# Two zero products of 256 columns ahead of the first and the second product of every chunk of a delta-rule recurrence

## Chip, cores, metric

One NeuronCore of a Trainium2 chip runs the whole program, in one launch. The metric is the device time of one execution in microseconds, the median of several; below it is the time of the slowest (here the only) core.

## What is computed

One inference step of a two-layer decoder, for a prompt of 1024 tokens and 8 sample rows. Layer 0 (a convolution branch and a sparse attention branch) is not touched by the change. Layer 1 is RWKV-7 time mixing: per head a 64x64 matrix state S is carried over the tokens.

```python
def rwkv_mixer(x, shift_prev, S0, mu, w_rkvz, w0, w1, w2, a0, a1, a2, k_k, k_a, r_k, gn_g, gn_b, w_out):
    ...
    r, k, v, z = jnp.einsum('nbtd,nde->nbte', xsh[:4], w_rkvz)
    ...
    def step(S, inp):
        r_t, w_t, k_t, v_t, kk_t, a_t = inp
        sa = jnp.einsum('bhvk,bhk->bhv', S, kk_t)
        S = S * w_t[:, :, None, :] - sa[..., None] * (kk_t * a_t)[:, :, None, :] + v_t[..., None] * k_t[:, :, None, :]
        return S, jnp.einsum('bhvk,bhk->bhv', S, r_t)
    S_fin, y = lax.scan(step, S0.astype(f32), (tm(r), tm(decay), tm(k), tm(v), tm(kk), tm(a)))
    ...
    out = (y.reshape(B, T, D_C).astype(x.dtype) * jax.nn.silu(z)) @ w_out
    return out, S_fin, x[:, -1]
```

The layer's output goes through a residual and a layer norm. 16 heads of 64, 1024 tokens.

## The kernel before

Phases A to C (layer 0) fill the first half of the time; phase D (`phase_d`, L1110 to L1883) is layer 1. The kernel is written as one long program in Python; a scheduler then orders the instructions of each engine by when it takes their inputs to be ready, and by their place in the program. TensorE (PE) runs its queue in that order.

Phase D has two kinds of work.

**The recurrence**, in 16 units: `units` is token group g (8 groups of 128 tokens) times half d (the heads in two halves of 8). A unit has two chunks (c = 0, 1) of 64 tokens. `s1` and `s2` prepare a unit's matrices and the pieces of an inverse, `joinUT` puts the inverse `UT` together with small products, and `s3` (L1533) is the serial chain. Per chunk, with the state and values in `SV`:

- L1547, the state products: 8 products `pA<-SV,AM` into the first half of the PSUM tile `pA`; L1549, a copy on VectorE (DVE) takes it out as `E`.
- L1552 and L1554: 8 products `pB<-AM,SV` and 2 products `pB<-SV,ident` start `pB`.
- L1559, the products with the inverse: 8 products `pA<-E,UT` into the second half of `pA`, on top of what is there; L1560 (ScalarE, ACT) and L1561 (DVE) copy the sum into `SV`.
- L1566 and L1568: 8 products `pB<-SV,BK` and 8 products `pB<-MRB,SV`; L1571 (DVE) makes the new state, L1572 (ACT) the output `Y`.

The trace shows all of these with the line of the helper `mm`, L1541, and twice as many records as products. After two chunks a norm follows (`yc` L1577, `sq` L1580, `var` L1585, logarithm and exponential L1586 and L1587, L1588 and L1589), and its result `sq` goes to memory; the last unit's stays on chip as `G.Y`. `pA` and `pB` have one buffer each, in a pool that the norm's `yc` and `var` use too.

**The filler**, generators in the list `F1`: projections `t_proj` (L1195 to L1197), and output projections `t_out` (L1807 to L1809) with the layer norm `ln_out`. `t_last` is the last output projection, for 256 tokens, with products at L1736 to L1738. It splits the weights into a high and a low part (L113 on ACT, L121 on GpSimd (POOL) or DVE), multiplies tile 0 (128 tokens) while the last unit runs, joins it with the residual (L1743) and norms it, waits for `G.Y`, prepares the last rows (`prep`, L1709), and multiplies tile 1 with weights that it kept on chip in the buffers `AM`, `SV`, `BK`, `MRB` of earlier units.

The loop at L1858 advances `s3` by one step, then the other generators, then the filler by `RATE` steps:

```python
            main = s3(g, d, JJ[u])
            for k in range(8):
                step(main)
                ...
                over = run(F1, RATE[u >= 6] - over)
```

So in the text of the program, filler products stand between any two steps of `s3`. A plain product has no tie to them, and the scheduler may issue it ahead of filler that was written before it. `tc.keep_in_program_order(...)` ties an instruction behind the last one of its engine that was written before it, as an order of issue and without a wait. `warm` (L1528) uses it in the last unit alone: after each of the three steps of a chunk, four zero products of 256 columns into a PSUM tile `pg` of their own, which nothing of the chain reads.

## Time and profile before

| | us |
|---|---|
| median of 3 runs | 2153.94 |
| lowest and highest | 2147.12, 2162.48 |
| the profiled execution | 2146.61 |
| its span, first to last instruction | 2144.6 |
| mean granted TensorE clock over the span | 0.889 |

The profile is of one execution. Starts are counted from the first instruction. The engines are PE (products), PEld (its weight loads), DVE, ACT, POOL, and SP, which issues most DMAs. A granted clock of 1.00 is 2.4 GHz and 0.50 is 1.2 GHz. The recurrence begins at about 1256 us; the last unit's first state products stand at 2087.48 us.

### The profile page before, as it was taken

How to read it: one execution, taken by the hardware profiler on the slowest of the kernel's cores; microseconds unless marked ns; L12 is line 12 of the kernel's file. 1: busy time of each engine (PE TensorE's matmuls, PEld its weight loads, DVE VectorE, ACT ScalarE, POOL GpSimd, SP SyncE). 2: the span in 40 equal slices, each digit the busy share in tenths (PEclk: the TensorE clock that was granted, in tenths of full speed). 3: DMA queues.
4: the chain of work that ended last, by engine and by line, in shares of the span. 5: the costliest groups of instructions: out<-in, count | busy, mean ns of one | idle time of the engine just before them, and what ended most of it. 6: DMA issues, size and time to landing. Idle time of an engine off the chain costs nothing. (4 is left out here: it accounts for less than half of the span.)

```text
span 2144.6 us, 41476 instructions
## 1 busy us (share of the span) xinstructions
PE 1826.6 (85%) x16106; PEld 1528.2 (71%) x16106; DVE 1474.2 (69%) x2550; ACT 1144.5 (53%) x2353; POOL 934.3 (44%) x765
## 2 busy tenths in 40 slices
PE   5997997848998998798878899899999886999875
PEld 5896886836776786575767898678688754976654
DVE  5998995467887788425645347873855899466864
ACT  3233224555665556356746555865874467455544
POOL 4667676564655455354534421242344435212211
PEclk9898998958998887798889899979789997999778
DMA  6424334440221112545656534443443445443443
GB/s 241 140 71 148 119 121 172 170 146 19 68 63 49 53 54 65 165 129 156 184 190 197 173 117 106 130 133 115 126 146 126 146 144 166 131 112 103 152 148 101
DMA packets 231519, 273.18 MB, mean 127 GB/s; under 512 B 71481, under 2 KB 171505, under 8 KB 227162
## 3 DMA queue, kind: packets, MB, share of 16 engines
q1 hardware_dynamic: 210136, 213.11, 32.5%
q0 software_dynamic: 7616, 41.52, 5.8%
q10 hardware_dynamic: 13570, 15.90, 2.1%
q8 instruction: 127, 2.08, 0.4%
q14 instruction: 70, 0.57, 0.1%
HBM read 210.37 MB, written 64.27 MB: 128 GB/s over the span
## 5 line engine op out<-in xcount | busy, mean ns | idle before, releaser
L121 POOL TENSOR_TENSOR wl<-w,wh 128x1024 fp32r<-128x1024 f32 x76 | 195.5, 2573 | 341.6 <-ACT wh L113 330.3
L1195 PE MATMUL mm<-xh,wh 128*128 128x256 f32 (+1 forms) x1024 | 308.2, 303 | 20.9 <-ACT og L1330 10.9
L1197 PE MATMUL mm<-xh,wl 128*128 128x256 f32 (+1 forms) x1024 | 300.5, 295 | 4.4 <-POOL wl L121 4.4
L1196 PE MATMUL mm<-xl,wh 128*128 128x256 f32 (+1 forms) x1024 | 302.8, 296 | 1.6 <-POOL xk L1215 0.8
L1195 PEld LDWEIGHTS mm<-xh,wh 128*128 128x128 f32 x1024 | 202.6, 199 | 33.4 <-ACT og L1330 13.7
L113 ACT ACTIVATE wh<-w 128x1024 fp32r<-128x1024 f32 (+1 forms) x122 | 126.0, 1034 | 165.5 <-DMA w<-in_w_fm 60.7
L1197 PEld LDWEIGHTS mm<-xh,wl 128*128 128x128 f32 x1024 | 202.9, 199 | 9.5 <-POOL wl L121 5.6
L1196 PEld LDWEIGHTS mm<-xl,wh 128*128 128x128 f32 x1024 | 204.3, 200 | 5.1 <-issue 2.1
L268 DVE SCALAR_TENSOR_TENSOR c<-U,cw,c 128x1024 f32<-128x1024 f32 x120 | 198.0, 1674 | 0.9
L604 POOL TENSOR_TENSOR Pl<-PT,Ph 128x512 fp32r<-128x512 f32 (+1 forms) x102 | 132.1, 1299 | 145.9 <-DVE Ph L603 114.9
L252 POOL TENSOR_TENSOR cbuf<-cbuf 128x256 f32<-128x256 f32 (+2 forms) x72 | 131.1, 1827 | 85.8 <-ACT cbuf L250 82.9
L217 PE MATMUL S<-xh,wh 128*128 128x344 f32 (+1 forms) x432 | 147.1, 341 | 23.3 <-ACT wh L113 19.3
L219 PE MATMUL S<-xh,wl 128*128 128x344 f32 (+1 forms) x432 | 145.6, 337 | 14.6 <-POOL wl L121 11.2
L218 PE MATMUL S<-xl,wh 128*128 128x344 f32 (+1 forms) x432 | 146.7, 340 | 3.8 <-POOL xl L121 3.7
L1223 POOL TENSOR_TENSOR xl<-xs,xh 128x520 fp32r<-128x520 f32 (+1 forms) x76 | 106.5, 1404 | 82.5 <-ACT xh L1222 80.7
L250 ACT ACTIVATE cbuf<-cbuf,wrow 128x256 f32<-128x256 f32 x192 | 79.3, 495 | 113.3 <-DMA cbuf<-in_ccmp,cix 72.1
L1219 DVE SCALAR_TENSOR_TENSOR xs<-xk,mu,xs 128x512 f32<-128x512 f32 x96 | 94.4, 989 | 55.2 <-ACT xs L1218 54.3
L217 PEld LDWEIGHTS S<-xh,wh 128*128 128x128 f32 (+1 forms) x432 | 85.4, 198 | 25.6 <-ACT wh L113 24.1
L562 DVE TENSOR_REDUCE nm<-S 128x1 f32<-128x640 f32 (+7 forms) x128 | 88.2, 698 | 19.8 <-PE S L558 19.0
L219 PEld LDWEIGHTS S<-xh,wl 128*128 128x128 f32 (+1 forms) x432 | 84.9, 197 | 19.7 <-POOL wl L121 13.4
L602 ACT ACTIVATE PT<-mm 128x512 f32<-128x512 f32 (+1 forms) x102 | 59.4, 586 | 57.9 <-PE mm L590 46.8
L218 PEld LDWEIGHTS S<-xl,wh 128*128 128x128 f32 (+1 forms) x432 | 84.9, 196 | 7.0 <-POOL xl L121 4.5
(666 smaller groups left out, 5305.1 us busy)
## 6 DMA issues: line engine op xcount, KB each, us to landing
w<-in_w_rkvz SPq DMA_DIRECT2D x64, 512.0 KB
w<-in_w_out SPq DMA_DIRECT2D x32, 512.0 KB
w<-in_w_fm SPq DMA_DIRECT2D x25, 512.0 KB
xk<-x1T SPq DMA_DIRECT2D x48, 260.0 KB
xk<-x1T SPq DMA_DIRECT2D x48, 256.0 KB
w<-in_w_out SPq DMA_DIRECT2D x16, 256.0 KB
x<-in_xp SPq DMA_DIRECT2D x8, 512.0 KB
x<-x ACTq DMA_DIRECT2D x8, 512.0 KB
```

Source lines behind the costliest of these rows:

```text
L113: nc.scalar.activation(hi, src, AF.Copy, **({} if scale is None else {"scale": scale}))
L121: e_lo.tensor_tensor(lo, src, hi, op=SUB)
L217: nc.tensor.matmul(dst, lhsT=wh[:, k, 0:n], rhs=xh[:, k, sl], start=k == 0, stop=False)
L218: nc.tensor.matmul(dst, lhsT=wh[:, k, 0:n], rhs=xl[:, k, sl], start=False, stop=False)
L219: nc.tensor.matmul(dst, lhsT=wl[:, k, 0:n], rhs=xh[:, k, sl], start=False, stop=k == 7)
L252: nc.gpsimd.tensor_tensor(bv[:, 0:n], bv[:, 0:n], bv[:, n:2 * n], op=ADD)
L268: e.scalar_tensor_tensor(c[:, i, 0:T], u[:, k:k + T], cwh[:, i, k:k + 1], c[:, i, 0:T], op0=MUL, op1=ADD)
L604: lambda: nc.gpsimd.tensor_tensor(Pl[:, 0:w], PT[:, 0:w], Ph[:, 0:w], op=SUB)]
L1195: nc.tensor.matmul(dst, lhsT=wh[:, k], rhs=xh[k][:, lo:hi], start=k == 0, stop=False)
L1196: nc.tensor.matmul(dst, lhsT=wh[:, k], rhs=xl[k][:, lo:hi], start=False, stop=False)
L1197: nc.tensor.matmul(dst, lhsT=wl[:, k], rhs=xh[k][:, lo:hi], start=False, stop=k == 7)
L1223: (nc.vector if early[0] and k % LD == 0 else nc.gpsimd).tensor_tensor(lo[k][:, 0:n], t[:, 0:n], hi[k][:, 0:n], op=SUB)
```

## The change

A helper `fillw` issues n zero products: `wz` (zeros, bf16, 128 columns of it as weights, 256 columns moved) into the tile that it is given, with `start=True`, each tied behind what was written before it. It is called with n = 2 in each of the 32 chunks at two places: on the first half of `pA` before the state products, and on the second half of `pA` before the products with the inverse. Both sets of products write to the same places after it, so each stands behind its pair. That is 64 pairs, 128 zero products. `wz` is made before `joinUT` now, with 256 columns for 512.

```diff
+        wz = late.tile([128, 256], BF, name="wz")
+        nc.gpsimd.memset(wz, 0.0)
+
+        def fillw(z, n):
+            for _ in range(n):
+                tc.keep_in_program_order(nc.tensor.matmul(z, lhsT=wz[:, 0:128], rhs=wz, start=True, stop=True,
+                                                          skip_group_check=True))
+
         def joinUT(J):
...
-        wz = late.tile([128, 512], BF, name="wz")
-        nc.gpsimd.memset(wz, 0.0)
-
         def warm(n):
...
             for c in range(2):
                 pA = py_.tile([128, 2, 4, 64], F32, name="pA")
                 pB = py_.tile([128, 2, 4, 64], F32, name="pB")
+                fillw(pA[:, 0].rearrange("p m t -> p (m t)"), 2)
                 for m, h, i in MH:
                     mm(pA[h, 0, m], AM[:, m, i, c], SV[:, m, i, c], m == 0)
...
                 if wn:
                     warm(wn)
                 yield
+                fillw(pA[:, 1].rearrange("p m t -> p (m t)"), 2)
                 for m, h, i in MH:
                     mm(pA[h, 1, m], UT[h, 2 * m + c], E[h, m], False)
```

Lines of the changed kernel: `fillw` is L1482, the helper `mm` L1546, `E` L1555, the copies into `SV` L1567 and L1568, the new state L1578, `yc` and `var` L1584 and L1592, `t_last`'s products L1743 to L1745 (so L1743 is a product there and the join of the kernel before; the join is now L1750).

The order of PE changes from the first unit to the end; the first unit's first state products stand in row 5658 before and in row 5876 now, of some 9000. Three places.

PE, second chunk of the second unit, the kernel before (waits in brackets name the engine waited for; `pg` belongs to `joinUT`):

```order
L1541 MATMUL pB<-SV,ident 64x256 x2
L1511 MATMUL pg<-U,AB 32x32 [waits DVE_49,PE_49,Activation_49]
L1511 MATMUL pg<-U,AB 32x32 x14
L1541 MATMUL pA<-E,UT 64x64 [waits DVE_49]
L1541 MATMUL pA<-E,UT 64x64 x7
```

The same kind of place in the changed kernel, with the filler products that stand ahead of it:

```order
L1195 MATMUL mm<-xh,wh 128x264
L1196 MATMUL mm<-xl,wh 128x264
L1482 LDWEIGHTS wz
L1482 MATMUL pA<-wz 128x256 [waits DVE_49]
L1482 LDWEIGHTS wz
L1482 MATMUL pA<-wz 128x256
L1546 MATMUL pA<-E,UT 64x64 x8
```

The wait for the copy `E` has moved from the first product with the inverse to the first zero product. It is so in 27 of the 32 pairs at this place; of the 32 pairs ahead of the state products 9 wait for ACT, 10 for PE itself, and the others for nothing.

PE, the last unit (g = 7, d = 1), the kernel before, from its first state products; `t_last`'s products into `mm` from `MRB` stand behind all that is shown, and behind the unit's norm (`yc` and `var`):

```order
L1585 MATMUL pB<-sq,cc 128x512
L1541 MATMUL pA<-SV,AM 64x64 x8
L1541 MATMUL pB<-AM,SV 64x64 x8
L1541 MATMUL pB<-SV,ident 64x256 x2
...
L1531 MATMUL pg<-wz 128x256
L1541 MATMUL pA<-E,UT 64x64 x8
...
L1541 MATMUL pB<-SV,BK 64x64 x8
L1541 MATMUL pB<-MRB,SV 64x64 x8
```

The changed kernel, the same unit's first products with the inverse:

```order
L1743 MATMUL mm<-MRB,xh 128x512
L1744 MATMUL mm<-MRB,xh 128x512
L1745 MATMUL mm<-MRB,xl 128x512
L1482 LDWEIGHTS wz
L1482 MATMUL pA<-wz 128x256
L1482 LDWEIGHTS wz
L1482 MATMUL pA<-wz 128x256
L1546 MATMUL pA<-E,UT 64x64 x8
```

All 48 products of `t_last`'s tile 0, up to the last pair of weights (in `MRB`), and the 24 of tile 1 that are written with them, now stand ahead of the last unit's first products with the inverse; the unit has its second chunk and the norm still to come. The other 24 products of tile 1 come last in both kernels.

DVE in the changed kernel, the same place, from the split of the last weights on (`big` is the residual, `st` the norm's sums, L1750 the join of tile 0; L1568 and L1578 are the chain's):

```order
L121 TENSOR_TENSOR MRB<-w,MRB 128x1024
L1750 SCALAR_TENSOR_TENSOR big,st<-big,mm 128x512 x2
L1685 TENSOR_SCALAR st<-st 128x1
L1568 COPY SV<-pA 64x4x64
L1690 TENSOR_SCALAR st<-st 128x1
L1698 SCALAR_TENSOR_TENSOR big<-big,st,w 128x1024
L1699 TENSOR_TENSOR st<-st 128x1
L1578 TENSOR_TENSOR SV<-pB,PC 64x4x64 x2
```

The join and a part of the layer norm of tile 0 now stand in the middle of the chain of the last unit; in the kernel before, the join of tile 0 stands behind that chain.

## Rows read from the trace of the kernel before

**Rows 1.** The page's first part: busy time, share, instructions.
```profile
PE 1826.6 (85%) x16106; PEld 1528.2 (71%) x16106; DVE 1474.2 (69%) x2550; ACT 1144.5 (53%) x2353; POOL 934.3 (44%) x765
```

**Rows 2.** Stretches: length, busy of PE, PEld, DVE, ACT, POOL; clock, DMA, GB/s.
```profile
1256.00:1586.00 330.00, 301.83 (x3882) 250.08 (x3879) 240.47 (x471) 229.12 (x496) 99.64 (x114) 0.89 0.43 125
1586.00:1750.00 164.00, 147.98 (x1780) 128.48 (x1779) 112.54 (x199) 85.86 (x178) 67.87 (x53) 0.97 0.47 144
1750.00:2090.00 340.00, 290.44 (x3658) 219.55 (x3658) 241.03 (x497) 198.24 (x400) 84.01 (x71) 0.86 0.43 134
2090.00:2125.00 35.00, 29.05 (x231) 20.01 (x229) 13.27 (x29) 15.19 (x27) 9.46 (x4) 1.00 0.35 113
```

**Rows 3.** Zero products of the last unit: their line, then PE in time.
```profile
L1531 PE MATMUL pg<-wz x24: 272/273/283, 2089.8 to 2106.5; 128*128 128x256 bf16 x24
...
2089.78 0.61 PE L1531 MATMUL pg<-wz 128*128 128x256 bf16 x4
2090.32 0.68 PE L1541 MATMUL pA<-E,UT 64*64 64x64 f32 x16
```

**Rows 4.** The chain's line L1541: records, then idle of PE before it.
```profile
L1541 PE MATMUL pA<-SV,AM x512: 222/222/369, 1270.4 to 2094.9; 128*64 128x64 f32 x171
...
L1541 PE MATMUL pA<-E,UT x512: 216/218/366, 1318.6 to 2101.9; 64*64 64x64 f32 x171
...
  DVE SV L1571: 11.5, 12
  DVE E L1549: 9.8, 7
```

**Rows 5.** PE in time, last unit and tile 0 of the last projection.
```profile
2094.01 1.14 PE L1541 MATMUL pA<-SV,AM 128*64 128x64 f32 x16
...
2096.13 0.61 PE L1531 MATMUL pg<-wz 128*128 128x256 bf16 x4
...
2108.88 1.02 PE L1577 MATMUL pA<-Y,cc 128*128 128x512 f32 x2
...
2122.54 0.39 PE L1736 MATMUL mm<-MRB,xh 128*128 128x512 f32 x1
...
2124.63 0.39 PE L1738 MATMUL mm<-MRB,xl 128*128 128x512 f32 x1
...
2129.39 0.40 PE L1738 MATMUL pa<-MRB,xl 128*128 128x512 f32 x1
```

**Rows 6.** The last weights of tile 0: SP, POOL and ACT in time.
```profile
2108.12 8.26 SPq L1186 DMA_DIRECT2D w<-in_w_out  x3
...
2120.90 1.04 ACT L113 ACTIVATE MRB<-w 128x1024 fp32r<-128x1024 f32 x1
...
2116.61 2.38 POOL L121 TENSOR_TENSOR BK<-w,BK 128x1024 fp32r<-128x1024 f32 x1 [0.58 <-ACT BK L113]
```

**Rows 7.** DVE and ACT in time, from the last unit's result to the end.
```profile
2120.30 0.61 DVE L1709 SCALAR_TENSOR_TENSOR xs<-sq,vec,xs 128x128 f32<-128x128 f32 x2
...
2131.52 0.68 DVE L1743 SCALAR_TENSOR_TENSOR big<-big,sm 128x512 f32<-128x512 f32 x1
...
2133.32 0.68 DVE L1743 SCALAR_TENSOR_TENSOR big<-big,pa 128x512 f32<-128x512 f32 x1
...
2139.29 1.28 DVE L1696 SCALAR_TENSOR_TENSOR big<-big,st,w 128x1024 f32<-128x1024 f32 x1
...
2126.04 1.15 ACT L1680 ACTIVATE og<-big,st 128x1024 bf16<-128x1024 f32 x1 [1.81 <-DVE st L1678]
...
2127.89 1.28 ACT L1685 ACT_TABLE_LOAD   x1
```

**Rows 8.** Stretches at the lower clock and one ahead of them, columns as above.
```profile
1420.00:1437.10 17.10, 16.09 (x128) 11.88 (x126) 14.49 (x28) 13.67 (x32) 6.70 (x8) 0.50 0.29 74
1498.50:1501.90 3.40, 2.04 (x43) 1.71 (x41) 0.31 (x2) 3.36 (x5) 1.47 (x2) 1.00 0.80 294
1501.90:1508.70 6.80, 5.61 (x61) 4.28 (x62) 6.19 (x8) 4.27 (x10) 4.21 (x4) 0.50 0.29 84
```

## The prediction

> **What bounds the kernel now.** I read the busy shares first, then stretches of phase D, then the lines of the chain, then the last 60 us in time, because there the program ends and a delay can no longer be made up.
>
> TensorE is busy for 85% of the span [rows 1], and for 91%, 90% and 85% of the three stretches from the first unit to 2090 us (301.83 of 330, 147.98 of 164, 290.44 of 340) [rows 2]. No other engine comes near, DVE at 69% being next [rows 1]. So in the body of phase D the queue of PE is nearly always full, and what is added to it costs about its length. It is not quite the bound everywhere: the chain waits for the new state (11.5 us in 12 places) and for the copy `E` (9.8 us in 7 places) [rows 4].
>
> The granted clock is 0.89, 0.97 and 0.86 in these stretches [rows 2]. There are two levels, 0.50 and 1.00, so the time at the lower one is twice what is missing: 2 x (0.11 x 330 + 0.03 x 164 + 0.14 x 340) = 178 us. Rows 8 show what such time looks like. In 1498.5 to 1501.9, still at 1.00, PE works for only 2.04 of 3.40 us; then it falls to 0.50 for 6.8 us, in which PE is busy for 5.61. Work at half the clock is lost capacity: with PE busy for 21.70 of the 23.90 us of the two cold stretches of rows 8, 178 us cost at most 178 x 0.91 / 2 = 81 us. That is the prize for keeping PE warm.
>
> From 2087 us on, two things run beside each other: the last unit's chain, and tile 0 of the last projection, which waits for its weights. The second is gated by DMAs and splits, not by PE: three loads of weights take SP from 2108.12 to 2116.38, because each waits for a buffer; the last weights are split by ACT at 2120.90 [rows 6], and tile 0's last product stands at 2124.63 [rows 5]. The chain is done earlier, at 2120.30, when the last rows are prepared [rows 7]. The end is 24.3 us after that (2144.6 - 2120.30).
>
> **The change part by part.** Zeros of half the width, made earlier: one instruction on POOL, nothing.
>
> *128 zero products.* The trace has the same product, 24 times, at 273 ns each; but four in a row begin at 2089.78 and the next product of the queue at 2090.32 [rows 3], so one takes 0.135 us of the queue at 2.4 GHz. 61 pairs stand ahead of the tail described below: 61 x 0.27 = 16.5 us, say 17, if PE is the bound at each. The least is 0, where PE waits anyway and the pair fits into the wait. The pair ahead of the state products may do that, since it mostly waits for nothing. The pair ahead of the products with the inverse can't: it now carries the wait for `E` in 27 of 32 places, so it starts when the wait is over and comes on top, for the 30 of them ahead of the tail 30 x 0.27 = 8.1 us. I take 8 us: that half, with the first half hidden.
>
> *The clock.* The same pairs add 0.27 us of products to a stretch. In the 3.40 us ahead of a fall, 2.04 busy would become 2.31 [rows 8]. I count no gain, and keep as bounds nothing and the whole 81 us.
>
> The trace shows that a stretch with little work is followed by the lower clock [rows 8]; the Trainium skill says the same on the page "TensorE: Matmul & The Clock Gate", in "Why this matters for your kernels", and advises to leave no gaps between bursts of products. By that advice the change would gain, up to the prize above, which is the first rival; against it stands that half of the pairs come after the gap and not in it.
>
> *The order in the tail.* This is the large term. A zero product is tied behind whatever PE work was written before it, and the chain's product writes the same half of `pA`, so the chain is tied too. In the last unit, the filler that was written between the state products and the products with the inverse is all of tile 0 of the last projection. Its last product ran at 2124.63 [rows 5], and what gates it is the row of loads and splits of rows 6, which doesn't depend on the last unit. So the products with the inverse move from 2090.32 [rows 3] to 2124.9. The rest of the chain then runs alone, and I add it up from before:
>
> - first products with the inverse to the next state products: 2094.01 - 2090.32 = 3.7 us [rows 3, 5]
> - state products to the end of the zero products behind them: 2096.13 + 0.54 - 2094.01 = 2.7 us [rows 3, 5]
> - the second products with the inverse to `yc`: 3.7 us again and one copy more, 4.5 us, an estimate
> - `yc` to the last rows: 2120.30 - 2108.88 = 11.4 us [rows 5, 7], in which two weight splits of 1.04 us [rows 6] stood on ACT: 9.3 us
> - three pairs of zero products: 0.8 us
> - the join and half the norm of tile 0, now ahead of the new state on DVE and ACT: a square of 1.15 and two table loads of 1.28 [rows 7], 3.7 us
>
> Sum 24.7 us. The last rows begin at 2149.6 instead of 2120.3, 29 us later. From there to the end some work is already done: tile 0's last products no longer stand between tile 1's, and tile 1's second join need not wait for tile 0's norm (2133.32, when its products were done at 2129.8 [rows 5, 7]). That gives back some 4 us. So the tail costs 25 us. Bounds: 17, if the loads and splits go 5 us faster without the chain beside them and the norm hides; 32, if nothing is given back and the waits for tile 0's norm are longer.
>
> What makes this hard is that PE's products don't overtake: PE stands idle for 9.8 us until `E` [rows 4], though the queue behind those products is long. The Trainium skill states it ("TensorE: Matmul & The Clock Gate", step by step, "LDWEIGHTS"): weight loads may be pulled ahead, products stay in program order. By that rule the chain is as late as the order has it, and the trace agrees; if products could pass, the tail would cost nothing and only the 8 us remain.
>
> *Sum.* Of the profiled execution, 2146.6 us (its span and 2.0 around it): 2146.6 + 25 + 8 = 2179.6, about 2180. The median of the runs shown lies 7.3 above that execution, and they spread over 15 us; I keep the sum and put the spread into the range.
>
> **The rivals.**
>
> - *The clock pays.* What a pair adds keeps PE above the fall in many places. For it: cold time costs up to 81 us, and 12 waits for the new state lie where a pair can run. Against it: 0.27 us is little, and half come after the wait. A saved stretch like 1501.9 gives back 2.8 us (5.61 / 2). Twelve would give 34: 2179.6 - 34 = 2146, the same as before. From 55 us back, two thirds of the prize, it is faster by over 1%, 2125 or below. Chance 0.15, of which a third on the fast side.
> - *The tail is hidden.* Tile 0 is through much earlier than 2124.6, so that the chain behind it is hardly late. For it: ACT and DVE are freed of the chain while the weights are split. Against it: SP is held by buffers until 2116.4 [rows 6]. Then 2146.6 + 8 = 2155, no change. Chance 0.15.
> - *The chain is held all along.* Ties like that of the tail hold every chunk behind filler that waits for weights, not only the last. For it: the first unit's state products stand some 200 rows later in PE's order. Against it: in the body the filler before a tie mostly is ready. Price: the 17 us of all pairs and the wait of one chunk in each unit, 1 us (11.5 / 12): 2146.6 + 25 + 17 + 16 = 2205. Chance 0.08.
> - *The changed order itself* moves waits of the body either way; I give it no mean and 10 us in the range.
>
> **How the numbers follow.** A measurement of this kernel can tell about 1%, some 21 us. The forecast, tail serial and pairs half hidden, has 0.62: 2180, from 2146.6 + 17 to 2146.6 + 32 + 17, that is 2164 to 2196. With the other order's 10 us on both sides the range is 2154 to 2206; it takes in the hidden tail and half of the held chain, and leaves out the larger gains of the clock. Slower by over 1%: 0.56 of the forecast (its lower end lies within 1%), and the held chain, 0.64. Faster by over 1%: 0.05. The rest, 0.31, within 1%.
>
> **What would show it.** In the changed profile, the last unit's products with the inverse begin more than 25 us after its state products, right behind the products from `MRB`; POOL and SP are done before them; the granted clock of the last 45 us is lower than 1.00; the body ends (tile 0's last product) within 10 us of 2124.6. The line of the zero products has 128 records, and 27 of 32 starts follow the copy `E`. It is wrong if the body's clock rises from 0.89 and 0.86 and that stretch shrinks by over 20 us, or if the last unit's chain is done before 2130.

## The result, and the profile after

The changed kernel took 2210.0 us (median of 4 runs, 2206.5 to 2215.1), beside 2150.5 us for the kernel before (4 runs, 2138.4 to 2162.5): a ratio of 1.0273, with a 95% interval from 1.0235 to 1.0312. It is slower, as forecast, by 59 us where 33 were forecast, and outside the range by 4 us. In what follows a ratio r, which each run has to executions of the kernel before taken along with it, is also told as (r - 1) x 2150 us, and its 95% interval stands in brackets behind it.

The profiled execution of the changed kernel took 2215.07 us, with a span of 2213.3, 68.7 more than the 2144.6 of before. It is the longest of its four, and that of before lies 4 us below its median, so the two profiles differ by 9 us more than the medians. The first part of its page, which answers to [rows 1]:

```profile
PE 1876.1 (85%) x16234; PEld 1560.1 (70%) x16234; DVE 1476.7 (67%) x2550; ACT 1149.5 (52%) x2355; POOL 932.3 (42%) x765
```

PE is busy for 49.5 us more. The 128 new products, at 0.135 us of the queue each, are 17 of these. The rest is old work that takes longer, and the clock column tells a part of why. These are the first three stretches of [rows 2] in the changed kernel (length, busy time and records of PE, PEld, DVE, ACT, POOL, then clock, DMA share, GB/s):

```profile
1256.00:1586.00 330.00, 294.39 (x3637) 241.83 (x3634) 222.49 (x430) 217.70 (x468) 94.31 (x108) 0.84 0.42 122
1586.00:1750.00 164.00, 152.31 (x1814) 132.39 (x1813) 98.58 (x184) 78.82 (x165) 56.75 (x47) 0.90 0.37 112
1750.00:2090.00 340.00, 301.35 (x3511) 227.60 (x3510) 242.81 (x491) 194.75 (x390) 92.88 (x82) 0.87 0.44 133
```

The clock fell from 0.89 to 0.84 and from 0.97 to 0.90 in the first two. In the first PE did less, 3637 records for 3882; in the second about as much, 1814 for 1780, and it was busy longer for it. So the chain falls behind early. The norm (its product `var`) of the fourth unit (unit 3) starts 4 us late, that of unit 4 already 44, that of unit 6 42, that of unit 14 46, and the last unit's 75.

The body, from 1256 us to the norm of unit 14, in one row of each kernel; first before, then after:

```profile
1256.00:2085.50 829.50, 735.75 (x9278) 595.63 (x9274) 593.61 (x1165) 508.79 (x1064) 251.51 (x237) 0.90 0.44 133
```

```profile
1256.00:2131.80 875.80, 777.26 (x9390) 622.02 (x9387) 590.66 (x1161) 513.05 (x1064) 247.76 (x237) 0.86 0.42 125
```

It is 46.3 us longer. PE's idle time is nearly the same, 98.5 for 93.8 us. The busy time is 41.5 us longer for 112 more records. The list of clock changes in the trace has 251 us at 0.50 in this stretch, for 171 before. PE is busy for 215 us in the first and 140 in the second. Were half of such time lost, that would be 37 us of the 46, but the rows leave less: of the 41.5 us of busy time, the body's 120 zero products are 16 at 0.135 us each, so the old work takes some 25 us longer. That is an estimate, and it is more than half of the 46.

**The tail** did what was forecast. PE in time, the last unit (L1743 to L1745 are the last projection, L1482 the new zero products), which answers to [rows 5]:

```profile
2136.30 0.79 PE L1546 MATMUL pA<-SV,AM 128*64 128x64 f32 x16
...
2170.39 0.63 PE L1745 MATMUL mm<-MRB,xl 128*128 128x512 f32 x1
2170.82 0.65 PE L1482 MATMUL pA<-wz 128*128 128x256 bf16 x2
2171.40 1.12 PE L1546 MATMUL pA<-E,UT 64*64 64x64 f32 x16
...
2177.81 1.14 PE L1546 MATMUL pA<-SV,AM 128*64 128x64 f32 x16 [2.16 <-DVE SV L1578]
...
2185.03 1.13 PE L1584 MATMUL pA<-Y,cc 128*128 128x512 f32 x2 [0.88 <-ACT Y L1579]
```

The first products with the inverse stand 35.1 us behind the state products, right behind tile 0's last product, for 2.8 us before. Tile 0's last product starts at 2170.39 us for 2124.63 [rows 5], 45.8 later: that is the body. From there to the end of the span it is 42.9 us for 20.0, 22.9 more: that is the tail. The two make up the 68.7. DVE begins the last rows at 2193.25, 21.9 us behind the first products with the inverse and 20.1 ahead of the end (24.3 before, 2144.6 - 2120.30 [rows 7]):

```profile
2193.25 0.61 DVE L1716 SCALAR_TENSOR_TENSOR xs<-sq,vec,xs 128x128 f32<-128x128 f32 x2
```

**The zero products** as a group of the changed kernel:

```profile
L1482 PE MATMUL pA<-wz x128: 269/283/437, 1312.1 to 2180.6; 128*128 128x256 bf16 x128
...
  issue: 10.9, 23
  DVE E L1555: 3.7, 4
```

There are 128, and idle time for the copy `E` is now ahead of them: 3.7 us in 4 places, for 9.8 in 7 ahead of the products with the inverse [rows 4] (`issue` is idle time for which the profile shows no wait). Their own length is 17 of the 68.7 us.

**Unit 4** is the first place where it falls far behind. PE in time, from its first state products to its first products with the inverse (L1245, L1246 and L1248 are the hidden products of `t_a`, one step of the filler without a break; L1222 and L1223 are their splits):

```profile
1497.87 0.69 PE L1546 MATMUL pA<-SV,AM 128*64 128x64 f32 x16
...
1505.41 0.80 PE L1245 MATMUL mm<-xh,wh 128*128 128x256 f32 x2 [3.56 <-ACT xh L1222]
...
1511.24 0.69 PE L1246 MATMUL mm<-xl,wh 128*64 128x256 f32 x2 [0.56 <-POOL xl L1223]
...
1525.96 0.42 PE L1248 MATMUL mm<-xh,wh 128*128 128x264 f32 x1
1526.18 0.65 PE L1482 MATMUL pA<-wz 128*128 128x256 bf16 x2
1526.77 1.12 PE L1546 MATMUL pA<-E,UT 64*64 64x64 f32 x16
```

The chain is held for 28.9 us (5.9 before), because the zero products are tied behind the whole of that step, and the step waits for splits. PE is not idle for most of that time: it is busy for 21.2 us, with the step and with other work that stands between its products, and 5.5 of the 7.7 idle us are waits for the splits. The two longest stretches at 0.50 among the first seven units begin in it and in a like place in unit 6 (held for 35.1 us, 8.9 before):

```profile
1505.10:1539.20 34.10, 27.70 (x272) 21.51 (x272) 30.70 (x54) 24.71 (x52) 14.65 (x17) 0.50 0.45 129
1658.70:1686.00 27.30, 27.07 (x268) 22.24 (x269) 17.18 (x44) 13.30 (x32) 2.54 (x2) 0.50 0.31 88
```

In the second of them PE is busy for 27.07 of 27.30 us, and the clock still stays at 0.50.

After this result two theories stood against each other. By the first, the ties hold the chain in the body as they do in the tail. By the second, the zero products cost more than their length. The experiments also had to tell whether the lower clock was part of it or only went along.

### The profile page after: what moved, and what is told of

Read it like the earlier page. It is cut to its first block, busy times and chain, and to the rows that moved or that the text cites. A ratio compares the mean times of both kernels' runs of the same rounds, so it can differ in the third digit from the quotient of the medians.

```text
span 2213.3 us, 41716 instructions
## 1 busy us (share of the span) xinstructions
PE 1876.1 (85%) x16234; PEld 1560.1 (70%) x16234; DVE 1476.7 (67%) x2550; ACT 1149.5 (52%) x2355; POOL 932.3 (42%) x765
## 4 chain that ended last, share of the span: by engine, by line
PE 21%; DVE 10%; ACT 7%; DMA 5%; issue 5%; SPq 2%; POOL 1%; DVEq 0%; ACTq 0%; POOLq 0%
PE mm L1195 4%; PE mm L1196 3%; PE mm L1197 3%; PE pB L1546 2%; DVE XT L1444 2%; PE pa L1407 1%; SPq L1474 1%; PE pA L1546 1%; DVE xs L1219 1%; DMA w<-in_w_out 1%; DMA xs<-sz 1%; ACT L1362 1%; ACT xs L1218 1%; DMA UT<-ud 1%; DMA ud<-XI 1%
## 5 line engine op out<-in xcount | busy, mean ns | idle before, releaser
L121 POOL TENSOR_TENSOR wl<-w,wh 128x1024 fp32r<-128x1024 f32 x76 | 188.9, 2486 | 348.0 <-ACT wh L113 320.6
L1195 PE MATMUL mm<-xh,wh 128*128 128x256 f32 (+1 forms) x1024 | 311.4, 305 | 25.9 <-ACT og L1330 11.5
L1197 PE MATMUL mm<-xh,wl 128*128 128x256 f32 (+1 forms) x1024 | 301.3, 295 | 4.8 <-POOL wl L121 4.8
L1195 PEld LDWEIGHTS mm<-xh,wh 128*128 128x128 f32 x1024 | 203.7, 199 | 42.2 <-ACT og L1330 14.3
L1197 PEld LDWEIGHTS mm<-xh,wl 128*128 128x128 f32 x1024 | 204.4, 200 | 7.8 <-POOL wl L121 5.9
L1223 POOL TENSOR_TENSOR xl<-xs,xh 128x520 fp32r<-128x520 f32 (+1 forms) x76 | 107.4, 1417 | 98.3 <-ACT xh L1222 96.5
```

The source lines that it names most:

```text
L121: e_lo.tensor_tensor(lo, src, hi, op=SUB)
L1195: nc.tensor.matmul(dst, lhsT=wh[:, k], rhs=xh[k][:, lo:hi], start=k == 0, stop=False)
L1197: nc.tensor.matmul(dst, lhsT=wl[:, k], rhs=xh[k][:, lo:hi], start=False, stop=k == 7)
```

## The experiments

### Which part of the change costs

The last unit's zero products taken out of the changed kernel (both calls):

```diff
-                fillw(pA[:, 0].rearrange("p m t -> p (m t)"), 2)
+                if not wn:
+                    fillw(pA[:, 0].rearrange("p m t -> p (m t)"), 2)
```

Expected: 

> The changed kernel without the zero products (and so without the ties) in the last unit's two chunks; the other 15 units keep theirs. If the tail is what the prediction says (the last unit's products with the inverse held behind the last projection's tile 0), 22 to 25 us are given back: 2185 to 2190 us, and the last unit's norm starts ahead of tile 0's last product again, with the body as late as in the changed kernel (some 46 us). If the last unit is late only because the body is, and the end follows the body's delay with no term of its own, 2205 to 2213.

Measured: 2191.0 us, 1.019 (1.015 to 1.0231), 18 us below the changed kernel. In the profile the last unit's state products and products with the inverse are 2.6 us apart again. The tail's term is real, and 41 us remain that are not of the tail.

The ties alone, put on the kernel before:

```diff
-                    mm(pA[h, 0, m], AM[:, m, i, c], SV[:, m, i, c], m == 0)
+                    tc.keep_in_program_order(mm(pA[h, 0, m], AM[:, m, i, c], SV[:, m, i, c], m == 0))
...
-                    mm(pA[h, 1, m], UT[h, 2 * m + c], E[h, m], False)
+                    tc.keep_in_program_order(mm(pA[h, 1, m], UT[h, 2 * m + c], E[h, m], False))
```

Expected: 

> The kernel before with no zero product added, but with the eight state products and the eight products with the inverse of every chunk tied in the order of the program, as the zero products are tied in the changed kernel. The changed kernel took 2210.0 us, the kernel before 2150.5. Theory A (the tie holds the chain behind filler that waits, in the body and in the tail; the zero products themselves cost little): 2190 to 2215 us, the start of the last unit's norm at 2170 us or later (2112.3 before, 2186.8 in the changed kernel), and more time at clock 0.50 than the 178 us of before. Theory B (the zero products cost their own length, 64 pairs of 0.27 us, and more where they follow a wait): the tail's 25 us alone remain, 2165 to 2180. Theory C (the zero products lower the clock by the little work that they are): 2145 to 2180 with cold time as before.

Measured: 2191.2 us, 1.0188 (1.015 to 1.0226). Without one zero product, 40 of the 59 us are there: the hold of unit 4 (28.4 us) and that of the last unit (35.9 us) too.

The reverse, the zero products without the tie:

```diff
-                tc.keep_in_program_order(nc.tensor.matmul(z, lhsT=wz[:, 0:128], rhs=wz, start=True, stop=True,
-                                                          skip_group_check=True))
+                nc.tensor.matmul(z, lhsT=wz[:, 0:128], rhs=wz, start=True, stop=True, skip_group_check=True)
```

Expected: 

> The changed kernel with all 128 zero products, but without the tie on them: the scheduler may place them, and the chain's products with them, ahead of filler that was written before. Theory A (the tie costs): 2145 to 2170 us, the body at most the 17 us of all pairs longer than before, and the last unit's norm started again about where it did before (2112 to 2135 us). Theory B (the zero products cost): 2190 or more in the body's part, that is before plus some 35 us, 2185 to 2195, with the tail's 22 us gone. Theory C (they change the clock): the mean clock of 1256 to 2090 us falls from 0.88 to 0.84 with the ties or without.

Measured: 2161.6 us, 1.0043 (1.0012 to 1.0075). All 128 zero products together cost 9 us if nothing is tied. The second theory falls. Nor do they harm the clock there: it is 0.90 in the body, as before (the row stands further down).

The pairs ahead of the products with the inverse alone:

```diff
-                fillw(pA[:, 0].rearrange("p m t -> p (m t)"), 2)
```

Expected: 

> The changed kernel with the tied pairs ahead of the products with the inverse alone; the pairs ahead of the state products are gone. Theory A with the harm at the products with the inverse (the filler written after the state products waits for its splits and weights): 2195 to 2212 us. Theory A with the harm at the state products: 2175 to 2185 us, the tail's 25 and few us of the body. Theory B: half of the body's 46 us, 2185 to 2190.

Measured: 2196.1 us, 1.0209 (1.0171 to 1.0247). Half of the pairs makes 45 of the 59 us. The tie at the products with the inverse does most of the harm.

### Where in the body

A tie in unit 4 alone, on the kernel before:

```diff
+            tie = tc.keep_in_program_order if (g, d) == (2, 0) else lambda x: x
...
-                    mm(pA[h, 1, m], UT[h, 2 * m + c], E[h, m], False)
+                    tie(mm(pA[h, 1, m], UT[h, 2 * m + c], E[h, m], False))
```

(and the same on the state products). Expected: 

> The kernel before, no zero product, with the state products and the products with the inverse tied in the order of the program in the unit of token group 2, half 0 (unit 4) alone. In every kernel with ties so far that unit's first products with the inverse came 28 to 32 us after its state products (6 before, 8 with untied zero products), and the unit's norm 35 to 44 us late, of which 16 were made up in the next unit. Theory A1 (the body's loss from ties is this one hold): 2165 to 2178 us, 15 to 27 over before, with the 28 us gap and unit 4's norm some 35 us late. Theory A2 (the ties of all units cost a little each): 2148 to 2158.

Measured: 2164.4 us, 1.0058 (1.0027 to 1.009), 12 us, with a gap of 33 us in unit 4: just under the range of the first reading, and above that of the second. That unit's norm is 31 us late in the profile, half of which is made up by the next one. The same condition with `(7, 1)`, the last unit alone:

Expected: 

> The kernel before, no zero product, with the state products and the products with the inverse tied in the last unit alone. If the tail's term is what the prediction worked out (the chain held behind tile 0 of the last projection, the body untouched): 2170 to 2178 us, 20 to 27 over before, the last unit's norm at 2150 instead of 2112, and less than 28 us between norm and end. If the tail is only long because the body was late already: 2148 to 2156.

Measured: 2172.3 us, 1.0082 (1.0048 to 1.0116), 18 us. PE in time, the last unit of that kernel (L1739 is tile 0's last product, L1542 the chain):

```profile
2093.12 1.12 PE L1542 MATMUL pA<-SV,AM 128*64 128x64 f32 x16
...
2126.38 0.39 PE L1739 MATMUL mm<-MRB,xl 128*128 128x512 f32 x1
2126.70 0.68 PE L1542 MATMUL pA<-E,UT 64*64 64x64 f32 x16
```

Tile 0's last product starts 1.8 us later than before (2124.63 [rows 5]), and the chain waits for it: the tail's mechanism by itself, with a body in which nothing is tied.

The changed kernel with the tie taken off in these two units:

```diff
-        def fillw(z, n):
+        def fillw(z, n, u):
+            tie = tc.keep_in_program_order if u not in ((2, 0), (7, 1)) else lambda x: x
             for _ in range(n):
-                tc.keep_in_program_order(nc.tensor.matmul(z, lhsT=wz[:, 0:128], rhs=wz, start=True, stop=True,
-                                                          skip_group_check=True))
+                tie(nc.tensor.matmul(z, lhsT=wz[:, 0:128], rhs=wz, start=True, stop=True, skip_group_check=True))
```

Expected: 

> The changed kernel with the ties on the zero products taken off in two units alone, unit 4 and the last; the zero products are all there. Theory A1 (of the ties, these two holds are what costs): 2160 to 2172 us, about the 2161.6 of the kernel without any tie. Theory A2 (the ties of all units cost a little each): 2178 to 2192.

Measured: 2175.9 us, 1.0103 (1.0069 to 1.0136): 22 us over before, between the two expectations. Freeing unit 4 is worth 19 us here (1.019 less 1.0103), and 13 us over the kernel without ties (1.0103 less 1.0043) stay with the others. The trace shows that these 19 us are not the price of one hold. With unit 4 free, unit 5 is held, for 30.3 us between its first state products and its first products with the inverse (5.0 in the changed kernel), behind other filler:

```profile
1557.32 1.12 PE L1546 MATMUL pA<-SV,AM 128*64 128x64 f32 x16
...
1587.58 0.68 PE L1546 MATMUL pA<-E,UT 64*64 64x64 f32 x16
```

Unit 6's norm is 39 us late there, for 42 in the changed kernel. The hold has moved one unit on.

Ties without zero products in the 14 other units (the condition `not in ((2, 0), (7, 1))`):

Expected: 

> The kernel before, no zero product, with the state products and the products with the inverse tied in 14 of the 16 units: all but unit 4 and the last. With ties in all 16 the time rose by 40 us (ratio 1.0188), with unit 4's alone by 12 (1.0058), with the last unit's alone by 18 (1.0082). If the parts add up, the other 14 units cost 40 - 12 - 18 = 10: 2155 to 2168 us. If unit 4 and the last are all, 2148 to 2155; above 2170 the parts do not add up.

Measured: 2193.8 us, 1.0183 (1.012 to 1.0246), 39 us, and this was the surprise. Without the ties of unit 4 and of the last unit it is as slow as with them. The parts of the ties don't add up. The trace of this kernel shows unit 5 held for 21.5 us between its first state products and its first products with the inverse (3.6 before, 4.8 with all ties), and unit 6 for 33.7 us between its first products with the inverse and its next state products (8.9 before, 26.8 with all ties). Over most of the second hold PE is at 0.50 and busy without a break:

```profile
1649.37:1680.09 30.72, 30.67 (x332) 25.09 (x330) 22.34 (x48) 16.96 (x39) 6.22 (x6) 0.50 0.29 86
```

What PE does in it, in time (L1407 prepares a later unit, `pg` belongs to the inverse):

```profile
1655.85 2.07 PE L1407 MATMUL pa<-AM,KBK 64*128 64x128 f32 x8
...
1671.86 1.06 PE L1511 MATMUL pg<-U,AB 32*32 32x32 f32 x32
...
1675.91 1.12 PE L1542 MATMUL pA<-SV,AM 128*64 128x64 f32 x16
```

Blocks of 24 filler products and more, one every 0.12 us at 1.00, end some 11 us ahead of it; in it only 23 of the 332 records are filler products (L1195 to L1197), and the rest is nearly all smaller. The kernel before mixes the two: in the 30 us shown next, 116 of 407 records are filler. That place as a row, then some of it in time:

```profile
1630.00:1660.00 30.00, 30.00 (x407) 25.30 (x408) 21.02 (x35) 16.86 (x34) 12.28 (x11) 1.00 0.31 97
```

```profile
1641.20 0.28 PE L1197 MATMUL mm<-xh,wl 128*128 128x256 f32 x1
...
1641.64 0.37 PE L1496 MATMUL pg<-UT,Gs 32*16 32x16 f32 x30
1641.95 0.33 PE L1541 MATMUL pB<-SV,BK 128*64 128x64 f32 x2
...
1642.41 0.71 PE L1407 MATMUL pa<-AM,KBK 64*128 64x128 f32 x8
```

It runs at 1.00 throughout, with eight records of L1407 in 0.71 us for 2.07. So there was a third theory (E in the expectations below; A2 is that every tie costs a little): the ties sort the work. Wide filler runs first, small products are left behind in a block, and there the clock stays at 0.50.

All ties again, with another order of the filler, to see whether `t_a`'s step is what holds unit 4:

```diff
-        F1 = [t_proj(1, "k", 1), t_sigma(1), t_proj(1, "r", 0), t_a(1), t_proj(1, "v", 2)]
+        F1 = [t_proj(1, "k", 1), t_sigma(1), t_a(1), t_proj(1, "r", 0), t_proj(1, "v", 2)]
```

(on the kernel with all ties and no zero product). Expected: 

> All ties and no zero product, as in the first experiment (2191 us), but the filler's list has t_a ahead of the projection r, so that t_a's hidden products, one uninterrupted step that waits for eight splits, are written in unit 2 instead of unit 4. If that step is what held unit 4, the 28 us between unit 4's first state products and its first products with the inverse fall below 12, and a gap of 20 us or more opens in unit 2, between its first products with the inverse and its next state products (11 us before): 2180 to 2205 us. If the gap belongs to unit 4 itself (its own matrices, copies or loads are late), it stays at 25 to 30.

Measured: 2208.6 us, 1.0249 (1.0195 to 1.0303), a little above what was expected. Unit 4's gap fell to 4.8 us, and one of 26.8 us opened in unit 2 (8.3 with the usual order). The step holds whichever unit it is written in. It isn't unit 4's own work that is late.

Unit 6 freed too (the condition `not in ((2, 0), (3, 0), (7, 1))`), no zero products:

Expected: 

> The ninth experiment (ties in 14 units, 2193.8 us, ratio 1.0183) with unit 6 free too. Theory E (the ties sort the work: wide filler runs first in a block, and the small products that stood among it run in a block of their own, in which the clock stays at 0.50; unit 6 is the largest such place, 30.7 us at 0.50 with TensorE busy throughout): that stretch is gone or below 14 us, and some 15 us of the time with it, 2170 to 2183 us. Theory A2 (every tie costs a little): 2188 to 2194 with the cold stretch moved, not gone.

Measured: 2166.2 us, 1.006 (1.0019 to 1.01). One unit's ties make 26 of the 39 us (the two ratios differ by 0.0123, with about 0.0075 either way, which is 16 us). Its stretch at 0.50 is 13.65 us, and the unit is held for 17.6 us. Both kernels from 1256 us to the norm of unit 14, first with unit 6 tied, then free:

```profile
1256.00:2124.50 868.50, 767.83 (x9306) 621.43 (x9304) 587.08 (x1163) 512.25 (x1067) 252.00 (x239) 0.86 0.42 125
```

```profile
1256.00:2104.50 848.50, 744.24 (x9307) 603.52 (x9305) 582.50 (x1167) 514.80 (x1071) 251.44 (x238) 0.89 0.44 131
```

With the same number of records, PE is busy for 23.6 us less, and idle no less (104.3 for 100.7 us). The whole difference of the body is in how long the same work took, at 0.89 for 0.86. Not all of it can be unit 6's. Up to 1634.5 us in the first and 1625.4 in the second PE's order is the same, and the two executions are 9.1 us apart there already. From there to the norm of unit 14:

```profile
1634.50:2124.50 490.00, 425.14 (x5081) 332.67 (x5080) 351.98 (x691) 269.36 (x542) 145.06 (x123) 0.86 0.42 127
```

```profile
1625.40:2104.50 479.10, 411.02 (x5086) 322.40 (x5085) 348.77 (x696) 272.93 (x547) 143.44 (x123) 0.89 0.45 136
```

What is left for unit 6's ties is 10.9 us of the body, with 14.1 us less of busy time, and 7.6 us behind it. In the same way the kernel with all ties and the one with ties in 14 units, whose order is the same up to unit 4, are 16.7 us apart at that place. So the time at which one profiled execution reaches a unit tells less than some 17 us.

Nor does the third theory tell all of the clock. With unit 6 free it fell at nearly the same place of the order and came back sooner, at 1654.27. PE in time around that moment:

```profile
1649.90 0.41 PE L1197 MATMUL mm<-xh,wl 128*128 128x256 f32 x1
...
1652.10 1.12 PE L1542 MATMUL pB<-AM,SV 64*64 64x64 f32 x16
1653.01 1.06 PE L1542 MATMUL pB<-SV,ident 64*64 64x256 f32 x4
...
1654.81 0.50 PE L1195 MATMUL mm<-xh,wh 128*128 128x256 f32 x2
```

The last filler product began 4 us ahead of the rise; between stand the chain's own products. The same products of 64x256 ran at 1660.61 in the long stretch of the kernel with unit 6 tied, and the clock stayed at 0.50. So which products bring it back, and when, the theory does not say.

Ties in units 7 to 14 alone (`7 <= 2 * g + d < 15`), no zero products:

Expected: 

> The kernel before with ties in units 7 to 14 alone. In the kernel with 14 tied units the seventh unit's norm is 38 us late and the fifteenth's 39: what is lost is lost early, where the filler is the projections and the matrices of the next units are made. Theory E and the trace: 2150 to 2162 us. Theory A2: half of the 39 us, 2168 to 2176.

Measured: 2152.0 us, 1.0005 (0.9971 to 1.0039). No difference that can be told (7 us either way). In that trace no unit from 7 to 14 has its first products with the inverse more than 1.1 us further behind its state products than before: these ties hold nothing.

And the changed kernel, with all zero products and the tie on them in units 7 to 14 alone:

Expected: 

> The changed kernel with all zero products, tied in units 7 to 14 alone. If the early ties and the last unit's are what costs beside the zero products, it is near the kernel with untied zero products (2161.6, ratio 1.0043): ratio 1.004 to 1.009, 2160 to 2172 us. If the zero products need a tie nowhere and cost with every tie, 1.012 or more, 2178 or later.

Measured: 2169.6 us, 1.0062 (1.0032 to 1.0093), near the 1.0043 without a tie. So the 59 us come apart along one row of kernels, each with fewer ties than the one before it: the last unit's 18 (1.0273 to 1.019), unit 4's 19 (to 1.0103), the other early units' 9 (to 1.0062), the late ones' 4 (to 1.0043), and the zero products' 9. (The second kernel of the row also lacks the last unit's four pairs.) Each difference has 7 to 12 us either way, so the late ties' 4 and, taken alone, the early units' 9 can't be told from none; unit 4's 19 and those 9 together, 28, can.

### The zero products and the clock

Four zero products for two, untied and then tied (`fillw(..., 4)` in both places):

Expected, untied: 

> Four zero products for two at each of the 64 places, 256 in all, none tied. With two, untied, the time was 2161.6 us, 11 over before, and the profiled execution showed 18.8 us more work of TensorE (counted at the full clock) for 128 x 0.135 = 17.3 us. Theory B (the zero products come on top nearly in full, since the queue is full at each): 17 more, 2174 to 2184, TensorE's work some 36 us above before. Theory D (they mostly fit into waits, and the 11 us come from the changed order): 2158 to 2168.

Measured: 2170.3 us, 1.0083 (1.0054 to 1.0113). The second 128 cost 9 us (9 either way) as the first did, half of their 17. The body of the two kernels, with two and with four:

```profile
1256.00:2107.50 851.50, 759.09 (x9438) 610.89 (x9438) 593.82 (x1168) 514.33 (x1075) 251.83 (x241) 0.90 0.44 130
```

```profile
1256.00:2118.50 862.50, 773.31 (x9566) 622.44 (x9564) 606.50 (x1168) 515.87 (x1074) 253.78 (x241) 0.91 0.43 129
```

PE is busy for 14.2 us more, 3.2 of which come out of idle time, and the clock is a little higher.

Expected, tied: 

> The changed kernel with four zero products for two at each place, tied. Two untied cost 9 us and two more untied 9 (ratios 1.0043 and 1.0083); two tied ones, put on top of the ties alone, cost 18 (1.0273 against 1.0188). Theory B (a tied pair stands behind the wait and comes on top in full, 61 x 0.27 = 17 us): 17 more than the changed kernel, ratio 1.034 to 1.037, 2222 to 2232 us. Theory D (the 18 are 9 of the pairs and 9 of an order that merely came out worse): 7 to 11 more, ratio 1.030 to 1.033. Theory C (more zero products, more of the full clock): no more than 2210 us, with less than the 270 us at clock 0.50 of the changed kernel.

Measured: 2232.5 us, 1.0399 (1.0335 to 1.0462), 27 us more than the changed kernel, with some 16 either way; their length would be 17. The clock of the body does rise, to 0.88 from 0.86, with 218 us at 0.50 for 251, and the kernel is slower all the same: theory C's gain is not there.

The kernel before without the 24 zero products of `warm` (`wn = 0`):

Expected: 

> The kernel before without the 24 tied zero products that it has in its last unit (written right behind the chain's own products, with no filler between, into a tile that the chain does not read). If zero products pay where the tie holds nothing (theory C in the tail), it is slower than before: 2156 us or more, with a lower clock after 2090 us. If they cost their length there too, 24 x 0.135 = 3 us: 2145 to 2152 us. Either is near what a measurement can tell.

Measured: 2150.1 us, 0.9986 (0.996 to 1.0012). These, tied behind the chain's own products, make no difference that can be told (from 9 us below to 3 above).

The third theory says that the block of small products keeps the low clock. So wide zero products were set into it, in the kernel with ties in 14 units, at the head of each of the four steps that join unit 7's inverse:

```diff
+        def wide(J, z):
+            for _ in range(4 if J is JJ[7] else 0):
+                nc.tensor.matmul(flat(z), lhsT=wz[:, 0:128], rhs=wz[:, 0:256], start=True, stop=True)
...
             pg = pq.tile([128, 8, 32], F32, name="pg")
+            wide(J, pg)
```

Expected: 

> The ninth experiment (2193.8 us) with 16 zero products of 256 columns more, untied, four at the head of each of the four steps that join unit 7's inverse, which are in the stretch of 30.7 us at clock 0.50. Theory E: the clock comes back to 1.00 within the stretch behind such a group, the stretch shrinks to below 20 us, and the time is the same or up to 10 us shorter though work was added: 2182 to 2194. If the stretch is slow for another reason (a wait, or the order as such), it stays at some 30 us and the zero products come on top at half the clock, 16 x 0.27 = 4 us: 2194 to 2200.

Measured: 2180.7 us, 1.0134 (1.0062 to 1.0205), against 1.0183 without them; the intervals overlap, so the time alone tells nothing. The trace tells more. The stretch at 0.50 is 10.24 us for 30.72, and what follows it runs at 1.00:

```profile
1643.59:1653.83 10.24, 8.30 (x60) 6.30 (x64) 7.05 (x18) 6.31 (x16) 1.51 (x3) 0.50 0.27 78
1653.83:1680.00 26.17, 22.76 (x315) 19.84 (x314) 22.12 (x46) 12.34 (x25) 6.94 (x6) 1.00 0.28 82
```

PE in time around the place where the clock rose (L1479 are the new products):

```profile
1648.68 2.07 PE L1407 MATMUL pa<-AM,KBK 64*128 64x128 f32 x8
1650.69 1.04 PE L1479 MATMUL pg<-wz 128*128 128x256 bf16 x4
...
1654.97 1.16 PE L1407 MATMUL pa<-AM,KBK 64*128 64x128 f32 x8
```

The clock rose 3.1 us after the four zero products began, and eight records of L1407 took 1.16 us for 2.07. The chain was still held, for 28.5 us. So in this one profile the low clock of that block went with what stood in it and not with the hold. That it was the zero products is not shown: it is one execution, products of the chain stand between them and the rise here too, and the order around the zero products, which are free to move, changed as well: in the 26 us at 1.00 behind the stretch 82 of the 315 records are filler.

Two more kernels put such groups into the kernel before: four products each for units 2 to 5, and two each for units 1 to 15.

Expected, four for units 2 to 5: 

> The kernel before with 64 zero products of 256 columns more, untied, four at the head of each of the four steps that join the inverse of units 2 to 5 (they run during units 1 to 4, where the kernel before has some 65 us at clock 0.50 with TensorE over 90% busy). Theory E: 64 x 0.135 = 8.6 us are added and more than half of the 65 us at 0.50 goes, worth 16 or more: 2140 to 2148 us. If the kernel before has too little to win at these places: 2152 to 2162, with the time at 0.50 before 1600 us above 50.

Measured: 2162.8 us, 1.0028 (0.9999 to 1.0057), with 58 us at 0.50 from 1256 to 1600 us for 72 before.

Expected, two for units 1 to 15: 

> The kernel before with two zero products at the head of each of the four steps that join the inverse, in units 1 to 15, 120 in all, untied: 16.2 us of work added. Theory E with a gain at every such step: 2140 to 2150 us and less than 140 us at 0.50 from 1256 us to the last unit's norm (174 before). If they cost like the untied ones in front of the chain's products (128 cost 9 us): 2157 to 2165.

Measured: 2176.9 us, 1.0095 (1.0065 to 1.0125). Both miss the expectation of a gain. Here is the second kernel up to 1600 us and from there to the norm of unit 14, and behind it the same of the kernel before:

```profile
1256.00:1600.00 344.00, 303.41 (x4001) 252.75 (x4001) 238.84 (x459) 227.16 (x499) 99.68 (x113) 0.94 0.43 122
1600.00:2108.50 508.50, 446.36 (x5356) 347.93 (x5355) 357.16 (x700) 282.09 (x564) 147.13 (x124) 0.87 0.43 133
```

```profile
1256.00:1600.00 344.00, 315.83 (x4019) 263.42 (x4016) 245.28 (x484) 242.97 (x523) 101.25 (x114) 0.90 0.43 126
1600.00:2085.50 485.50, 419.92 (x5261) 332.21 (x5260) 348.33 (x681) 265.82 (x542) 150.26 (x123) 0.90 0.45 137
```

The early clock rises from 0.90 to 0.94, and the later one falls from 0.90 to 0.87. Up to 1600 us the time at 0.50 is 41 us for 72, and up to the norm of unit 14 it is 169 us, for 171 before. So the time at 0.50 can be shorter with zero products, but here they bought no time: the norm of unit 5, at about 1605 us, is 10 us late already, the clock lost behind 1600 us what it won up to there, and the kernel costs 20 us more. No kernel of this study is faster than the one before by more than can be told; why the later clock fell was not tried.

## Why the prediction went wrong

- **The zero products, 8 us.** Right in its number: 9 us without ties (interval 3 to 16) and 13 with ties that hold nothing (7 to 20). The reason given, that the half ahead of the state products would fit into waits, is not shown: with the untied zero products PE's idle time in the body is 92.4 us, for 93.8 before, and of the second 128 only 3.2 us came out of idle time. So the number was partly luck.
- **The tail, 25 us.** Right in its mechanism and close in size: 22.9 us in the profile and 18 by the runs, twice (the last unit freed, and tied alone). The chain's pieces, worked out as 3.7 + 3.7 to the next state products, came to 6.4 us, those from there to `yc`, 2.7 + 4.5, to 7.2, and from `yc` to the last rows 8.2 us for 9.3. From the last rows to the end 4.2 us were given back, for 4. The granted clock of the last 45 us is 0.77, lower than 1.00 as was said (0.88 before). The products with the inverse stand right behind the products from `MRB`, as was said they would.
- **The changed order of the body.** This is the step that failed: "The changed order itself moves waits of the body either way; I give it no mean and 10 us in the range." It cost 28 us by the runs (1.019 to 1.0062 for the ties of units 0 to 6, with 11 either way), and tile 0's last product, which was to be within 10 us of 2124.6, stands at 2170.39. The tail had been worked out as a tie behind filler that waits; the same reasoning applies to unit 4 and unit 6, and the prediction waved it off with "in the body the filler before a tie mostly is ready". In units 7 to 14 that is so (1.0005). In the early units it is not, and one step of filler without a break, behind eight splits, holds whichever unit it is written in.
- **The clock, nothing.** The bounds were "nothing and the whole 81 us", both on the side of a gain. The loss wasn't seen: with 80 us more at 0.50 than before, the body's old work took some 25 us longer, of the 46 in the profile. The freed unit 6 shows the same without any zero product: behind the first place where the two orders differ, 14.1 us of busy time for the same records.
- **The rivals.** "The chain is held all along" came nearest, at 0.08 and 2205 us. Its sum, 25 for the tail, 17 for all pairs and 16 for waits, was near in total by luck: the chain is held in some of the early units and not all along, the pairs cost 9 to 13, and what the body loses is hardly idle time (4.8 us), but longer work. "The clock pays" and "the tail is hidden" failed.

What stays open: the share of the clock in the 19 us of unit 4 and in the 9 of the other early units, since the profiled execution without the last unit's ties lies 6.5 us below its median, and that with the late ties alone 6.6 us above. Nor do the runs tell fully why the ties of unit 4 and of the last unit add nothing to those of the other 14 (1.0188 for 1.0183, with intervals of 8 to 13 us either way); that a hold taken away in unit 4 comes back in unit 5 and in a longer one of unit 6 is a part of it. And which products bring the clock back from 0.50 is not shown.

## What to carry to other kernels

An order of issue that is pinned to the text of the program also pins the instruction behind everything written before it: look up, at each such place, what that is and what it waits for, and do so in the body as carefully as at the end. Take away one hold and look where the next one is, before the difference is put down to it. A stretch in which TensorE is busy is not yet a stretch in which it is fast; read the granted clock beside the busy share. Before a difference between two profiles is put down to an edit, look how far apart they are at the first instruction that the edit moves. Before zero products are added for the clock, count whether their own length comes back over the whole program and not only in the stretch.

## What the runs showed of the hardware

TensorE stayed at 0.50 for 30.72 us while it was busy for 30.67 of them, mostly in small products; in the kernel before such products, mixed with wide ones, ran for 30 us at 1.00. The Trainium skill ("TensorE: Matmul & The Clock Gate", "Part 1: The HAM clock gate") says that the clock is set by how busy the engine has been of late, and speaks of idle gaps as what lowers it. Here the measurement differs: there is hardly a gap between PE's records in that stretch (though the profile models where a product ends), and the clock rose only at 1680.09, just behind the next filler product, at 1679.56. In the kernel with unit 6 free it rose at 1654.27, among the chain's own products and 4 us behind the last filler product, so filler alone is not what decides. What does was not measured.

At the lower clock eight records of L1407 took 2.07 us, for 0.71 among wide filler at the higher one, nearly three times as long. The clock is not all of that. In the 2.07 us they start one behind another, 0.21 us apart; at 1.00, in the kernel with zero products in the join, they do so 0.11 us apart and take 1.16 us. In the 0.71 us they start two at a time (1642.41 and 1642.42, 1642.63 and 1642.63). So the clock makes a factor of 1.8 of it, and the rest goes with how the products start.
